# The start of a hybrid encoder layer: how the first operands are loaded, ordered and split

## The chip, the cores and the metric

The kernel runs on one core of a Trainium2 chip. Time is device time in microseconds (us) of one execution of the program; less is better. Engines are named as in the profile: PE is TensorE (PEld its weight loads), DVE VectorE, ACT ScalarE, POOL GpSimd, SP SyncE, which here only issues DMAs. A "q" behind an engine's name is its instruction queue, where DMAs are issued.

## The reference

One layer of a streaming encoder over 512 tokens of width 1024, in float32. Of its three parts (a SwiGLU feed-forward, a mixer of attention and a gated recurrence, a second SwiGLU), only the first is touched here:

```python
def rms_norm(x, g):
    xf = x.astype(jnp.float32)
    y = xf * lax.rsqrt(jnp.mean(xf * xf, axis=-1, keepdims=True) + RMS_EPS)
    return (y * g.astype(jnp.float32)).astype(x.dtype)

def swiglu(x, w1, w3, w2):
    return (jax.nn.silu(x @ w1) * (x @ w3)) @ w2
...
    f = swiglu(rms_norm(h, ffn1_pre_g[l]), ffn1_w1[l], ffn1_w3[l], ffn1_w2[l])
    h = h + 0.5 * rms_norm(f, ffn1_post_g[l])
```

w1 and w3 are 1024 x 2816, w2 is 2816 x 1024.

## The kernel before, in words

Matmuls take two-part operands. Each float32 operand is split into a high part in a reduced format (`fp32r`), made by a copy on ACT, and a low part, the rest, made by a subtraction on DVE. A product is then three matmuls: high x high, low x high and high x low.

**Units.** Columns of w1 and w3 are handled in tiles of 128, each laid out in memory as one 128 x 1024 tile (512 KB): eight blocks k of 128 x 128, one per 128 rows of the weight. A unit is one such tile times the normalized x, transposed: for each k three matmuls of 128 x 512, 24 in all (`mm_feat`, L194). Units come in turns, w1 tile 0, w3 tile 0, w1 tile 1, w3 tile 1 and so on; counted in this `order` from 0, units 0, 1 and 2 are the beginning, unit 3 is w3 tile 1, unit 4 w1 tile 2, unit 5 w3 tile 2. After twelve units the remaining tiles go in pairs through a scheme with fewer products (`Pairs`, L478), whose operands are prepared in parts by `prep`; part 0 makes sums of raw weights (L518 to L521), part 1 splits the first raw tile, part 2 splits sums.

**The norm is applied late.** The first units multiply the weights with x^T scaled by the gain only (`uT`: its high part on ACT, L665, its low part on DVE, L666). The factor of each token comes from the sums of squares of the x rows, which are loaded once more as the residual `h` (four tiles of 512 KB, `h_load`, L94; squares on ACT, L680; the factor in `rstd4`, L244). It is put on diagonals (`dgs`, L686), multiplied with a tile of ones on PE (L700) and copied by ACT to `Rb` (L701). `silu_mul` (L426) then scales the units' results by Rb on DVE.

**The beginning, before.** DVE fills a warm-up tile of 128 x 512 with zeros and PE runs nine matmuls on it (L621 to L625). ACT runs a tiny activation, then issues the load of x^T tile 0 (256 KB, `load_x(0, act)`). SP issues the vector of gains and biases (`vec`), then for each pair of k (kp) a quarter of the raw tiles of units 0, 1 and 2 (128 KB each, `load_w`) and two x^T tiles; for kp = 0 in the order weight 0, weight 1, weight 2, x^T tile 1. Then the raw tiles of units 3 and 4, the four residual tiles and the first two raw tiles of the pairs. The stage at L660 goes through k: for an even k split a quarter of unit 0's weights, scale x^T tile k, split units 1 and 2, and then nine matmuls, three per unit, units in turn.

**Order of the work.** The program order of each engine is as written: every engine takes its queue in order, and what waits holds up all behind it. Tiles live in 42 slots of 4 KB per partition (`slot`); a load into a slot that is in use waits on SP for the slot's last reader. `dma_to(n)` issues the raw loads of all units before n, `split_to(n)` their splits; `get(nm, i, ahead, rawahead)` (L161) asks for both, by default so that two units ahead are split and three more loaded. `point()` runs due work that was put off by `later`.

**After the beginning (L676 to L704), before.** Split units 3 and 4; squares of the four residual tiles; the factor; a tiny activation that brings in the table for Silu; the diagonals; part 0 of the first pair on DVE; then unit 3 through `unit` (its `get` splits unit 5 and requests raw tiles up to unit 8), two small products on PE (one for a table of position biases, whose result `erow` POOL writes to memory as `bias_scr`, L696), the products for Rb, Rb on ACT, parts 1 and 2 of the pair and the first two `silu_mul`.

Of the kernel before, what the change touches and what calls it, by code (L numbers as in the profile page):

```python
# [11 lines left out]
F32R = mybir.dt.float32r  # L12
AF = mybir.ActivationFunctionType
ALU = mybir.AluOpType

P = 128
SEQ = 512
D = 1024
KT = D // P
D_FF = 2816  # L20
FT = D_FF // P
NT = SEQ // P
# [9 lines left out]
V_CW, V_CB, V_BA, V_BX, V_LAM, V_BG, V_G1, V_SINK, V_N = 0, 32, 40, 48, 56, 64, 80, 88, 104  # L32
# [19 lines left out]
def hybrid_layer(ctx: ExitStack, tc: tile.TileContext, a: dict, out: bass.AP):  # L52
    nc = tc.nc
    act, dve, pool, pe, sp = nc.scalar, nc.vector, nc.gpsimd, nc.tensor, nc.sync
# [8 lines left out]
    def slot(shape, dt=F32, name="s"):  # L63
        uid[0] += 1
        return sb.tile(shape, dt, tag="slot", name=f"{name}_{uid[0]}")

    def bank(name="ps"):
        uid[0] += 1
        return pp.tile([P, 512], F32, tag="ps", name=f"{name}_{uid[0]}")
# [5 lines left out]
    def f32(ap):  # L75
        return ap.bitcast(F32)
# [3 lines left out]
    vec = cp.tile([P, V_N], F32, name="vec")  # L80
# [13 lines left out]
    def h_load(src):  # L94
        for t in range(NT):
            h[t] = slot([P, D], name="h")
            sp.dma_start(out=h[t], in_=src[t])
# [51 lines left out]
    def split_to(n):  # L149
        while st["split"] < min(n, len(order)) and st["split"] not in paired:  # L150
            k = st["split"]
            dma_to(k + 1)
            r = raws.pop(k)
            hi = slot([P, D], F32R, name="whi")
            lo = slot([P, D], F32R, name="wlo")
            act.activation(hi, r, AF.Copy)
            dve.tensor_tensor(out=lo, in0=r, in1=f32(hi), op=ALU.subtract)  # L157
            pairs[k] = (hi, lo)
            st["split"] += 1
# [47 lines left out]
    def unit(nm, i, **kw):  # L207
        w = get(nm, i)
        ps = bank("f")
        mm_feat(ps, w, **kw)  # L210
        return ps
# [32 lines left out]
    def rstd4(s4):  # L244

        v, r, e, r2 = (small(NT, x) for x in ("v", "r", "e", "r2"))
        dve.tensor_scalar(out=v, in0=s4, scalar1=D * EPS, scalar2=None, op0=ALU.add)
        act.activation(r, v, AF.Abs_reciprocal_sqrt)
        dve.tensor_tensor(out=e, in0=r, in1=r, op=ALU.mult)
        dve.tensor_tensor(out=e, in0=e, in1=v, op=ALU.mult)  # L250
        dve.scalar_tensor_tensor(out=r2, in0=e, scalar=-3.0, in1=r, op0=ALU.add, op1=ALU.mult)
        return r2, r
# [353 lines left out]
    NS = 3  # L606
# [5 lines left out]
    def load_x(k, q=sp):  # L612
        q.dma_start(out=xts[k // 2][:, k % 2, :], in_=a["xT"][k * P : (k + 1) * P, :])

    def load_w(u, kp):
        nm, i = order[u]
        c = slice(kp * 2 * P, (kp + 1) * 2 * P)
        sp.dma_start(out=raw3[u][:, c], in_=a[nm][i * P : (i + 1) * P, c])


    warm = slot([P, 512], F32R, name="warm")  # L621
    dve.memset(f32(warm), 0.0)
    psw = bank("w")
    for _ in range(WARM):
        pe.matmul(psw, warm[:, :P], warm, start=True, stop=True)  # L625


    tiny = small(4, "tiny")
    dve.memset(tiny, 1.0)
    act.activation(tiny, tiny, AF.Abs_reciprocal_sqrt)  # L630
    load_x(0, act)
    sp.dma_start(out=vec, in_=a["vec"])
    for kp in range(KT // 2):
        load_w(0, kp)
        if kp:
            load_x(2 * kp)
        load_w(1, kp)
        load_w(2, kp)
        load_x(2 * kp + 1)
    dma_to(NS + 2)  # L640
    h_load([a["x"][t * P : (t + 1) * P, :] for t in range(NT)])

    hid, X1 = Hidden(), {}
    pairs_a = Pairs("w1a", "w3a", NC1, X1, hid)
# [12 lines left out]
        hi, lo = pair3[u]  # L657
        split2(hi[:, c], lo[:, c], raw3[u][:, c])

    for k in range(KT):  # L660
        if k % 2 == 0:
            split_first(0, k // 2)
        g = vec[:, V_G1 + k : V_G1 + k + 1]
        xk = xts[k // 2][:, k % 2, :]
        act.activation(uT[:, 0, k, :], xk, AF.Copy, scale=g)  # L665
        dve.scalar_tensor_tensor(out=uT[:, 1, k, :], in0=xk, scalar=g, in1=f32(uT[:, 0, k, :]), op0=ALU.mult, op1=ALU.subtract)  # L666
        if k % 2 == 0:
            split_first(1, k // 2)
            split_first(2, k // 2)
        s_ = slice(k * P, (k + 1) * P)  # L670
        for (hi, lo), p_ in zip(pair3, ps):
            pe.matmul(p_, hi[:, s_], uT[:, 0, k, :], start=k == 0, stop=False)
            pe.matmul(p_, lo[:, s_], uT[:, 0, k, :], start=False, stop=False)
            pe.matmul(p_, hi[:, s_], uT[:, 1, k, :], start=False, stop=k == KT - 1)
    del raw3, pair3, hi, lo
    split_to(NS + 2)  # L676
    s4 = small(NT, "s4")
    for t in range(NT):
        junk = slot([P, D], name="junk")
        act.activation(junk, h[t], AF.Square, accum_out=s4[:, t : t + 1])  # L680

    r, q = rstd4(s4)
    act.activation(tiny, q, AF.Silu)
    dgs = slot([P, NT, P], name="dgs")
    for t in range(NT):
        dve.tensor_scalar(out=dgs[:, t, :], in0=ident, scalar1=r[:, t : t + 1], scalar2=NEWT, op0=ALU.mult, op1=ALU.mult)  # L686
    pairs_a.prep(0, 0, dve)
    ps.append(unit("w3a", 1))

    pse = bank("e")  # L690
    pe.matmul(pse[:N_HEADS, : NREL + 1], oh[:, NREL + 1 :], oh[:, : NREL + 1], start=True, stop=True)
# [7 lines left out]
    for t in range(NT):  # L699
        pe.matmul(psr[:, t * P : (t + 1) * P], ones, dgs[:, t, :], start=True, stop=True)  # L700
    act.activation(Rb, psr, AF.Copy)  # L701
    pairs_a.prep(0, 1)
    hid.f += [silu_mul(ps[0], ps[1], Rb), silu_mul(ps[2], ps[3], Rb)]
    pairs_a.prep(0, 2)  # L704
# [226 lines left out]
    for i in range(8):  # L931
        ps = unit("wg", i)
# [261 lines left out]

CONV_AT = (0, 1, 2, 4, 5, 6, 8, 10)
RG_AT = (7, 11, 13, 15, 17, 19, 21, 23)
WARM = 9
ATT_STEP = 2.2
ATT_LAG = (1, 1, 4, 1, 3, 1)
RG_LAG = 2  # L1200
# [63 lines left out]
```

## Time and profile before

| | |
|---|---|
| median of three executions | 1135.56 us (1135.35 to 1135.70) |
| the profiled execution | 1135.67 us |
| its span, first to last instruction | 1133.8 us |
| mean granted PE clock | 0.998 |

An engine's rows read: start and length in us, engine, line, operation, tiles written and read, shapes, and in brackets the engine's idle time before it and what ended that. A row of the stretches gives the stretch, its length, then the busy time of PE, PEld, DVE, ACT and POOL with instruction counts, the granted clock, the share of the DMA engines in use and GB/s. A row of waits names who waited for whom: us in total, times, longest. A row of DMA issues ends with the number of issues, the size of one and the us from issue to landing.

### The profile page before, as it was taken

What the parts mean: (1) busy time and instruction counts of PE and PEld (TensorE: products, weight loads), DVE (VectorE), ACT (ScalarE), POOL (GpSimd) and SP (SyncE); (2) the same over time, 40 slices, a digit from 0 to 9 for tenths busy, and PEclk for the clock granted to TensorE, in tenths of its full rate; (3) what the DMA queues carried; (4) which work ended last, traced back from release to release, by engine and by line L of the source; (5) the groups of instructions that cost most, each with busy time, mean ns of one, the idle gap of its engine ahead of it and who ended that gap; (6) DMA issues with size and microseconds to landing.
All of it is one profiled execution on the core that took longest, in us unless ns stands there. A gap on an engine that the chain in (4) does not pass through costs nothing.

```text
span 1133.8 us, 17339 instructions
## 1 busy us (share of the span) xinstructions
PE 1125.3 (99%) x6763; PEld 1003.5 (89%) x6763; DVE 790.1 (70%) x1181; ACT 585.2 (52%) x1042; POOL 353.8 (31%) x265
## 2 busy tenths in 40 slices
PE   9999999999999999999999999999999999999997
PEld 7889999988889987888888888889999999998886
DVE  5997889885436747695678865767899777975313
ACT  6445555574324349844655663356555555574211
POOL 0148678500000000001555643000965566700000
PEclk9999999999999999999999999999999999999999
DMA  9953223264313311234122333531323332255101
GB/s 343 157 135 112 93 95 112 76 222 151 110 56 135 144 56 57 75 95 148 56 78 90 93 95 112 185 111 38 113 94 94 112 112 76 94 197 172 40 19 56
DMA packets 36945, 124.94 MB, mean 110 GB/s; under 512 B 4416, under 2 KB 6208, under 8 KB 36864
## 3 DMA queue, kind: packets, MB, share of 16 engines
q1 hardware_dynamic: 34272, 115.15, 30.3%
q0 software_dynamic: 2448, 8.43, 4.0%
q8 instruction: 53, 0.87, 0.3%
q10 hardware_dynamic: 144, 0.26, 0.1%
q14 instruction: 28, 0.23, 0.1%
HBM read 116.50 MB, written 7.33 MB: 109 GB/s over the span
## 4 chain that ended last, share of the span: by engine, by line
PE 93%; DVE 3%; ACT 2%; issue 1%; DMA 0%; SPq 0%; DVEq 0%
PE c L475 11%; PE c L474 11%; PE c L473 11%; PE f L202 10%; PE f L201 10%; PE f L203 10%; PE acc L220 8%; PE acc L221 8%; PE acc L219 8%; PE pt L1067 1%; PE s L1031 1%; PE s L1030 1%; PE tr L310 1%; PE o L1083 1%; PE o L1084 1%
## 5 line engine op out<-in xcount | busy, mean ns | idle before, releaser
L201 PE MATMUL f<-uT,whi 128*128 128x512 f32 (+1 forms) x504 | 184.2, 365 | 0.0
L202 PE MATMUL f<-uT,wlo 128*128 128x512 f32 (+1 forms) x504 | 183.0, 363 | 0.4 <-DVE wlo L157 0.3
L203 PE MATMUL f<-uT,whi 128*128 128x512 f32 (+1 forms) x504 | 182.6, 362 | 0.0
L219 PE MATMUL acc<-whi,hT 128*128 128x512 f32 x352 | 137.1, 390 | 0.0
L220 PE MATMUL acc<-wlo,hT 128*128 128x512 f32 x352 | 137.0, 389 | 0.0
L221 PE MATMUL acc<-whi,hT 128*128 128x512 f32 x352 | 136.9, 389 | 0.0
L474 PE MATMUL c<-Xh,wlo 128*128 128x256 f32 x432 | 122.3, 283 | 0.0
L475 PE MATMUL c<-Xl,whi 128*128 128x256 f32 x432 | 122.3, 283 | 0.0
L473 PE MATMUL c<-uT,whi 128*128 128x256 f32 x432 | 122.3, 283 | 0.0
L474 PE MATMUL c<-uT,wlo 128*128 128x256 f32 x432 | 122.3, 283 | 0.0
L475 PE MATMUL c<-uT,whi 128*128 128x256 f32 x432 | 122.3, 283 | 0.0
L473 PE MATMUL c<-Xh,whi 128*128 128x256 f32 x432 | 122.3, 283 | 0.0
L192 DVE TENSOR_TENSOR wlo<-S,whi 128x1024 fp32r<-128x1024 f32 x72 | 118.2, 1642 | 3.6 <-ACT whi L191 3.2
L202 PEld LDWEIGHTS f<-uT,wlo 128*128 128x128 f32 x504 | 95.2, 189 | 15.8 <-DVE wlo L157 1.6
L201 PEld LDWEIGHTS f<-uT,whi 128*128 128x128 f32 x504 | 95.1, 189 | 15.8 <-issue 1.4
L203 PEld LDWEIGHTS f<-uT,whi 128*128 128x128 f32 x504 | 95.1, 189 | 14.8
L473 PEld LDWEIGHTS c<-Xh,whi 128*128 128x128 f32 x432 | 82.9, 192 | 0.0
L474 PEld LDWEIGHTS c<-Xh,wlo 128*128 128x128 f32 x432 | 82.9, 192 | 0.0
L473 PEld LDWEIGHTS c<-uT,whi 128*128 128x128 f32 x432 | 82.9, 192 | 0.0
L474 PEld LDWEIGHTS c<-uT,wlo 128*128 128x128 f32 x432 | 82.9, 192 | 0.0
L475 PEld LDWEIGHTS c<-uT,whi 128*128 128x128 f32 x432 | 82.9, 192 | 0.0
L475 PEld LDWEIGHTS c<-Xl,whi 128*128 128x128 f32 x432 | 82.9, 192 | 0.0
(309 smaller groups left out, 2703.8 us busy)
## 6 DMA issues: line engine op xcount, KB each, us to landing
raw_w2a<-in_w2a_dram SPq DMA_DIRECT2D x22, 512.0 KB, 3.7
raw_w1b<-in_w1b_dram SPq DMA_DIRECT2D x22, 512.0 KB, 4.2
raw_w3b<-in_w3b_dram SPq DMA_DIRECT2D x22, 512.0 KB, 4.2
raw_w2b<-in_w2b_dram SPq DMA_DIRECT2D x22, 512.0 KB, 4.1
raw_w3a<-in_w3a_dram SPq DMA_DIRECT2D x21, 512.0 KB, 4.5
raw_w1a<-in_w1a_dram SPq DMA_DIRECT2D x20, 512.0 KB, 4.5
raw_wg<-in_wg_dram SPq DMA_DIRECT2D x16, 512.0 KB, 3.7
raw_xr<-in_xr_dram SPq DMA_DIRECT2D x8, 512.0 KB, 4.7
```

What stands on the lines that cost most here:

```text
L192: dve.tensor_tensor(out=lo, in0=src, in1=f32(hi), op=ALU.subtract)
L201: pe.matmul(ps[:, c0:c1], wh[:, s], h_, start=k == 0, stop=False)
L202: pe.matmul(ps[:, c0:c1], wl[:, s], h_, start=False, stop=False)
L203: pe.matmul(ps[:, c0:c1], wh[:, s], l_, start=False, stop=k == KT - 1)
L219: pe.matmul(acc[n], x[:, 0, c], wh[:, s], start=first, stop=False)
L220: pe.matmul(acc[n], x[:, 0, c], wl[:, s], start=False, stop=False)
L221: pe.matmul(acc[n], x[:, 1, c], wh[:, s], start=False, stop=last)
L310: pe.transpose(ps[:, k * P : (k + 1) * P], hg[:, kk * P : (kk + 1) * P], ident)
L473: pe.matmul(ps, wh[:, s], xh, start=first, stop=False, skip_group_check=True)
L474: pe.matmul(ps, wl[:, s], xh, start=False, stop=False, skip_group_check=True)
L475: pe.matmul(ps, wh[:, s], xl, start=False, stop=k == 3, skip_group_check=True)
L1030: pe.matmul(o, lq, KS[g][:, 0, k0 : k0 + n], start=True, stop=False)
```

## The change

The warm-up tile becomes 128 x 128, is filled by POOL, and is read four times over as the moving operand of the warm-up matmuls, of which there are seven. x^T tile 0 is loaded in two column halves, one issued by SP, one by ACT, ahead of everything else; `vec` goes behind the half on ACT. x^T tile 1 goes ahead of weight 2; in later rounds the first x^T tile goes ahead of all three weights. The residual tiles are requested ahead of unit 4's raw tile.

For k = 0 the steps are written out: x's high part first on ACT; unit 0's weights wholly on DVE (the copy too); units 1 and 2's high parts on ACT; the nine matmuls in another order. From k = 1 the order is as before.

Behind the beginning, only unit 3 is split ahead of the squares; unit 4 is split behind the factor, unit 5 behind Rb; unit 3's `get` looks one unit ahead instead of two.

```diff
-    warm = slot([P, 512], F32R, name="warm")
-    dve.memset(f32(warm), 0.0)
+    warm = slot([P, P], F32R, name="warm")
+    pool.memset(f32(warm), 0.0)
     psw = bank("w")
+    wide = bass.AP(tensor=warm.tensor, offset=warm.offset, ap=[warm.ap[0], [0, 4], [1, P]])
     for _ in range(WARM):
-        pe.matmul(psw, warm[:, :P], warm, start=True, stop=True)
-
+        pe.matmul(psw, warm, wide, start=True, stop=True)
+
+
+    for q, c0 in ((sp, 0), (act, 256)):
+        q.dma_start(out=xts[0][:, 0, c0 : c0 + 256], in_=a["xT"][:P, c0 : c0 + 256])
+    act.dma_start(out=vec, in_=a["vec"])
 
     tiny = small(4, "tiny")
     dve.memset(tiny, 1.0)
     act.activation(tiny, tiny, AF.Abs_reciprocal_sqrt)
-    load_x(0, act)
-    sp.dma_start(out=vec, in_=a["vec"])
     for kp in range(KT // 2):
-        load_w(0, kp)
         if kp:
             load_x(2 * kp)
+        load_w(0, kp)
         load_w(1, kp)
+        if not kp:
+            load_x(1)
         load_w(2, kp)
-        load_x(2 * kp + 1)
+        if kp:
+            load_x(2 * kp + 1)
+    dma_to(NS + 1)
+    h_load([a["x"][t * P : (t + 1) * P, :] for t in range(NT)])
     dma_to(NS + 2)
-    h_load([a["x"][t * P : (t + 1) * P, :] for t in range(NT)])
...
-    for k in range(KT):
+    def x_hi(k):
+        act.activation(uT[:, 0, k, :], xts[k // 2][:, k % 2, :], AF.Copy, scale=vec[:, V_G1 + k : V_G1 + k + 1])
+
+    def x_lo(k):
+        dve.scalar_tensor_tensor(
+            out=uT[:, 1, k, :], in0=xts[k // 2][:, k % 2, :], scalar=vec[:, V_G1 + k : V_G1 + k + 1],
+            in1=f32(uT[:, 0, k, :]), op0=ALU.mult, op1=ALU.subtract)
+
+    def mm_first(k, u, w, x):
+        pe.matmul(
+            ps[u], pair3[u][w][:, k * P : (k + 1) * P], uT[:, x, k, :],
+            start=k == 0 and w == x == 0, stop=k == KT - 1 and x == 1)
+
+
+    (hi0, lo0), c = pair3[0], slice(0, 2 * P)
+    x_hi(0)
+    dve.tensor_copy(hi0[:, c], raw3[0][:, c])
+    dve.tensor_tensor(out=lo0[:, c], in0=raw3[0][:, c], in1=f32(hi0[:, c]), op=ALU.subtract)
+    for u in (1, 2):
+        act.activation(pair3[u][0][:, c], raw3[u][:, c], AF.Copy)
+    x_lo(0)
+    for u in (1, 2):
+        dve.tensor_tensor(out=pair3[u][1][:, c], in0=raw3[u][:, c], in1=f32(pair3[u][0][:, c]), op=ALU.subtract)
+    for u, w, x in ((0, 0, 0), (0, 1, 0), (1, 0, 0), (2, 0, 0), (0, 0, 1), (1, 0, 1), (2, 0, 1), (1, 1, 0), (2, 1, 0)):
+        mm_first(0, u, w, x)
+    for k in range(1, KT):
         if k % 2 == 0:
             split_first(0, k // 2)
-        g = vec[:, V_G1 + k : V_G1 + k + 1]
-        xk = xts[k // 2][:, k % 2, :]
-        act.activation(uT[:, 0, k, :], xk, AF.Copy, scale=g)
-        dve.scalar_tensor_tensor(out=uT[:, 1, k, :], in0=xk, scalar=g, in1=f32(uT[:, 0, k, :]), op0=ALU.mult, op1=ALU.subtract)
+        x_hi(k)
+        x_lo(k)
         if k % 2 == 0:
             split_first(1, k // 2)
             split_first(2, k // 2)
-        s_ = slice(k * P, (k + 1) * P)
-        for (hi, lo), p_ in zip(pair3, ps):
-            pe.matmul(p_, hi[:, s_], uT[:, 0, k, :], start=k == 0, stop=False)
-            pe.matmul(p_, lo[:, s_], uT[:, 0, k, :], start=False, stop=False)
-            pe.matmul(p_, hi[:, s_], uT[:, 1, k, :], start=False, stop=k == KT - 1)
-    del raw3, pair3, hi, lo
-    split_to(NS + 2)
+        for u in range(NS):
+            for w, x in ((0, 0), (1, 0), (0, 1)):
+                mm_first(k, u, w, x)
+    del raw3, pair3, hi0, lo0
+    split_to(NS + 1)
     s4 = small(NT, "s4")
     for t in range(NT):
         junk = slot([P, D], name="junk")
         act.activation(junk, h[t], AF.Square, accum_out=s4[:, t : t + 1])
 
     r, q = rstd4(s4)
+    split_to(NS + 2)
     act.activation(tiny, q, AF.Silu)
...
     pairs_a.prep(0, 0, dve)
-    ps.append(unit("w3a", 1))
+    w = get("w3a", 1, ahead=1)
+    ps.append(bank("f"))
+    mm_feat(ps[3], w)
...
     act.activation(Rb, psr, AF.Copy)
+    split_to(NS + 3)
     pairs_a.prep(0, 1)
...
-WARM = 9
+WARM = 7
```

## The prediction, before the changed kernel was run

> **What bounds the kernel now.** I read the page's shares and chain first, then the stretches and the waits of TensorE (PE), then the first 10 us row by row.
>
> ```profile
> PE 1125.3 (99%) x6763; PEld 1003.5 (89%) x6763; DVE 790.1 (70%) x1181; ACT 585.2 (52%) x1042; POOL 353.8 (31%) x265
> ...
> PE 93%; DVE 3%; ACT 2%; issue 1%; DMA 0%; SPq 0%; DVEq 0%
> ```
> ```profile
> 28.30:40.00 11.70, 11.70 (x56) 9.32 (x56) 10.70 (x14) 7.99 (x11) 1.03 (x1) 1.00 0.96 195
> 40.00:60.00 20.00, 19.70 (x87) 16.02 (x86) 19.83 (x29) 6.05 (x7) 2.40 (x1) 1.00 0.97 126
> 60.00:100.00 40.00, 40.00 (x280) 37.54 (x279) 35.04 (x35) 21.62 (x33) 25.77 (x14) 1.00 0.42 125
> ```
> ```profile
> PE w L625 <- DVE tiny L629: 1.4, 1, 1.4
> PE f L202 <- DVE wlo L157: 0.3, 1, 0.3
> ```
>
> PE is busy 99% and holds 93% of the chain. In the stretches (length, then busy time of PE, weight load, DVE, ACT, POOL) the reader should see that only the first 60 us matter: from 60 to 100 us PE has no gap. And between 28 and 60 us DVE is as full as PE (10.70 of 11.70, 19.83 of 20.00). PE's list of waits has two rows: before its first matmul, and once for a low half made by DVE. So a microsecond won at the start reaches the end only if DVE arrives a microsecond earlier at that second row.
>
> The start, from the timeline:
>
> ```profile
> 0.73 0.39 SPq L632 DMA_DIRECT2D vec<-in_vec_dram  x1
> ...
> 1.18 0.42 SPq L618 DMA_DIRECT2D raw_first<-in_w1a_dram  x1
> ...
> 1.45 4.21 PE L625 MATMUL w<-warm 128*128 128x512 f32 x9 [1.45 <-DVE tiny L629]
> 1.46 0.37 ACTq L613 DMA_DIRECT2D xt<-in_xT_dram  x1
> ...
> 2.59 0.43 SPq L613 DMA_DIRECT2D xt<-in_xT_dram  x1
> ...
> 3.79 0.42 ACT L191 ACTIVATE whi<-raw_first 128x256 fp32r<-128x256 f32 x1 [1.57 <-DMA raw_first<-in_w1a_dram]
> ...
> 4.62 0.72 ACT L665 ACTIVATE uT<-xt,vec 128x512 fp32r<-128x512 f32 x1 [0.42 <-DMA xt<-in_xT_dram]
> ...
> 5.46 0.74 PE L672 MATMUL f<-uT,whi 128*128 128x512 f32 x1
> ...
> 6.60 0.39 PE L672 MATMUL f<-uT,whi 128*128 128x512 f32 x1
> ...
> 6.83 0.40 PE L673 MATMUL f<-uT,wlo 128*128 128x512 f32 x1
> ...
> 7.14 0.72 ACT L665 ACTIVATE uT<-xt,vec 128x512 fp32r<-128x512 f32 x1 [1.10 <-DMA xt<-in_xT_dram]
> ...
> 7.90 0.75 DVE L666 SCALAR_TENSOR_TENSOR uT<-xt,vec,uT 128x512 fp32r<-128x512 f32 x1 [1.09 <-ACT uT L665]
> ...
> 9.05 0.40 PE L672 MATMUL f<-uT,whi 128*128 128x512 f32 x1
> ```
>
> The first useful matmul starts at 5.46, when x's high half is made (4.62 + 0.72). Nine warm-ups take 4.21 us, at most 0.47 each; from 6.60 to 6.83 the step is 0.23. I number the useful matmuls from 0: number 12, at 9.05, is the first after which PE has no gap until 57 us. **Its place is the measure of the start**: what it gains, PE gains up to 57 us.
>
> **The change at the start.** Issue to landing, each row from the DMA view of a window about one issue:
>
> ```profile
> vec<-in_vec_dram SPq DMA_DIRECT2D x1, 52.0 KB, 1.8
> ```
> ```profile
> xt<-in_xT_dram ACTq DMA_DIRECT2D x1, 256.0 KB, 3.1
> raw_first<-in_w1a_dram SPq DMA_DIRECT2D x1, 128.0 KB, 2.6
> ```
> ```profile
> raw_first<-in_w3a_dram SPq DMA_DIRECT2D x1, 128.0 KB, 3.3
> raw_first<-in_w1a_dram SPq DMA_DIRECT2D x1, 128.0 KB, 3.5
> ```
>
> SP's first five issues (0.73 to 2.59) stand 0.46 us apart. Before: vec 0.73, weight 0 at 1.2, weight 1 at 1.65, weight 2 at 2.1, x tile 1 at 2.6; x tile 0 goes out on ACT at 1.46. After: SP sends half of x 0 at 0.73, weight 0 at 1.2, weight 1 at 1.65, x 1 at 2.1, weight 2 at 2.6; ACT sends the other half at 0.73 and vec at about 1.1, then loads its table, which ends about 2.9 and hides behind the landings.
>
> Half a tile alone is bounded by vec's 1.8 us below and the whole tile's 3.1 above: x 0 lands between 2.5 and 3.8. I take 3.5, nearer the upper row, because both halves are under way together. vec now lies behind a half: 2.9 to 4.2 by the same two rows, I take 3.7, and that starts the scaling of x, 0.9 us earlier than 4.62. Weight 0 lands as before, 3.8, or a little later beside the halves: 4.0.
>
> [...]
>
> DVE now makes weight 0's high half. There is no row of that copy at this size; the nearest is twice as wide:
>
> ```profile
> L849 DVE CAST xcs<-xc_t x8: 418/420/423, 396.9 to 451.4; 128x512 fp32r<-128x512 f32 x8
> ```
>
> So 0 to 0.42 us, I take 0.35: ready at 4.35, the low half 0.42 later; x's high half at 3.7 + 0.72 = 4.42. **Matmul 0 starts about 4.5**, 0.9 earlier, still at the slow rate; 1 and 2 follow to 5.4. Matmul 3 needs the high half of weight 2, and PE takes its queue in order. Weight 2 has gone behind x 1: 948 KB are now issued up to and including it, just what was issued before up to x 1, which landed at 7.1 (the wait of ACT's row at 7.14 ends with it); when 128 KB less x 1 lay ahead, it landed at 5.6 (2.1 + 3.5). These are the bounds, 5.6 and 7.1. The flow now begins earlier with full transfers and weight 2 is half of x 1's size, so I take the lower end, 5.8. ACT's copy (0.42) gives matmul 3 at 6.25, then nine steps of 0.23 to number 12, and a little for the end of the slow rate: 8.4. By the other limit, ACT scales x 1 from 6.2 to 6.9, DVE's low half takes 0.75, so number 11 can start at 7.7 and does not bind. **PE's gain at number 12: 9.05 - 8.4 = 0.65 us**; by the bounds 0.85 to -0.55.
>
> The smaller warm tile costs nothing visible: POOL fills 128x128 where DVE filled 128x512.
>
> ```profile
> 0.73 0.20 POOL masks.py:197 MEMSET ident<- 128x128 f32 x1 [0.29 <-POOLq L1252]
> ```
>
> Warm-ups begin about 1.0 instead of 1.45; seven of them end about 4.2, before matmul 0. Identity and the ones tile go 0.2 us later on POOL; their readers are the diagonals and products just ahead of Rb.
>
> **The change at 16 to 58 us.** The rows on which it hangs:
>
> ```profile
> 27.38 0.69 DVE L518 TENSOR_TENSOR S<-raw_w1a 128x512 f32<-128x512 f32 x1 [0.87 <-DMA raw_w1a<-in_w1a_dram]
> ...
> 28.61 1.06 ACT L156 ACTIVATE whi<-raw_w3a 128x1024 fp32r<-128x1024 f32 x1 [2.15 <-DMA raw_w3a<-in_w3a_dram]
> ...
> 30.05 1.22 DVE L157 TENSOR_TENSOR wlo<-raw_w3a,whi 128x1024 fp32r<-128x1024 f32 x1
> 30.18 0.60 ACT L701 ACTIVATE Rb<-r 128x512 f32<-128x512 f32 x1
> 30.34 1.03 POOL L696 DMA_DIRECT2D bias_scr<-erow  x1 [27.64 <-ACT erow L693]
> 30.67 1.05 ACT L191 ACTIVATE whi<-raw_w1a 128x1024 fp32r<-128x1024 f32 x1
> 31.76 1.23 DVE L192 TENSOR_TENSOR wlo<-raw_w1a,whi 128x1024 fp32r<-128x1024 f32 x1 [0.50 <-ACT whi L191]
> 32.90 0.69 DVE L433 TENSOR_TENSOR sw<-f,Rb 128x512 f32<-128x512 f32 x1
> ...
> 47.13 1.23 DVE L157 TENSOR_TENSOR wlo<-raw_w1a,whi 128x1024 fp32r<-128x1024 f32 x1
> ...
> 56.63 1.22 DVE L157 TENSOR_TENSOR wlo<-raw_w3a,whi 128x1024 fp32r<-128x1024 f32 x1
> ...
> 57.90 0.50 PE L202 MATMUL f<-uT,wlo 128*128 128x512 f32 x1 [0.30 <-DVE wlo L157]
> ```
> ```profile
> 31.70:57.90 26.20, 25.90 (x115) 21.12 (x114) 25.50 (x37) 11.10 (x14) 2.40 (x1) 1.00 0.97 125
> ```
>
> The residual tiles move ahead of weight tile 4 (units counted from 0), so the squares on ACT and the factor come about 1.2 us earlier; but the factor's consumer waits for PE anyway. Tile 4's split moves behind it, to about 24 to 26 us; PE needs it only after the product that Rb copies (30.18 - 0.65). Both cost nothing. In DVE's queue tile 4's split delays the diagonals by 1.2 us, before the sums at 27.38 that wait for a DMA: hidden.
>
> The step that costs is **tile 5's split**, moved behind Rb. Before, DVE made its low half at 30.05 to 31.27, in time that it would otherwise have idled, since the next product waited for Rb and a copy on ACT until 31.76. After, ACT makes Rb, then tile 5's high half, then the pair's; DVE waits from about 30 until tile 5's copy, at 31.76 - 0.65, makes its low half there, and only then the pair's. One step of this kind is 1.14 us (31.76 to 32.90). Behind it DVE is full to the row that PE waits for: 25.50 of 26.20 us. Nothing there can take up 1.14 us. So the low half at 56.63 comes 1.14 - 0.65 = 0.49 us later, and PE, which already waited for it, with it. From there PE is without a gap, so the end moves as that matmul does.
>
> **Sum:** span 1133.8 + 0.49 = 1134.3; the profiled execution took 1135.67, 1.87 more than its span and 0.11 above the median 1135.56. On the median: 1135.56 + 0.49, **1136.1 us**. It is not measurable: 0.2% (2.3 us), about what a measurement of this kernel can tell from no change, is four times as much.
>
> **Rivals.**
> (a) *DVE's delay is absorbed.* For it: DVE idles 0.70 us in that window. Against: the idle parts follow ACT work that moves along. PE would keep its 0.65: 1134.9.
> (b) *Weight 2 lands late*, the start does not do what it says. At 7.1, matmul 3 starts at 7.55 and number 12 at 9.6: 0.55 lost, plus 1.14: 1137.25. For it: the bytes ahead; against: the earlier flow.
> (c) *The slow rate lasts longer.* Here the rate rose by 6.60, 5.15 us after the first warm-up. PE now idles about 0.3 us before matmul 0 and 0.8 before matmul 3. If the count began anew at matmul 0, the slow rate would hold to 9.65; from 6.25 on half of 3.4 us is lost, 1.7, and 0.49 + 1.7 gives 1137.75. It decides from 0.65 us of lost rate on, where it outweighs the gain at the start. [...] The trace agrees with a change of rate, with 0.23 us after 6.60; whether a short gap resets it no row shows.
> (d) *A tile is caught behind the bias transfer.* One weight load issued at 33.0 beside it took
>
> ```profile
> raw_w3a<-in_w3a_dram SPq DMA_DIRECT2D x1, 512.0 KB, 23.4
> ```
>
> to land. That transfer now starts some 1.2 us earlier, since its row no longer queues behind the copy at 28.61, and tile 8 is requested one call later. Tile 8's low half is DVE's row at 47.13. If tile 8, issued at about 24, took as long, it would land at 47.4 and with ACT's copy (1.06) delay that row by 1.3 us: 1137.4; if it landed with the quoted one, at 56.4, by ten: 1146. Against: it is issued some 5 us before the transfer.
>
> **How the numbers follow.** Forecast 0.48 (its own range 1135.4 to 1136.9), (a) 0.24, (b) 0.13, (c) 0.11, (d) 0.04. The range takes in (a), (b) and the lower part of (c), 1134.6 to 1137.7; it leaves out half of (c), (d), and the lowest fifth of (a). Slower by over 0.2% begins at 1137.83: (d), half of (c) and a little of (b), 0.11. Faster by over 0.2% (below 1133.3) would need both the whole gain and the removal of the stall at 57 us with more: 0.03. Within: 0.86.
>
> **What would show it.** Matmul 0 near 4.5 and a gap before matmul 3 that a DMA of the third weight ends; number 12 near 8.4; DVE idle before tile 5's low half near 31; PE's wait at the tenth unit grown from 0.3 to about 1.5 us. If that wait has not grown, the DVE step was wrong; if number 12 is later than 9, the start was.

## The result and the profile after

The changed kernel took 1139.36 us (median of six executions, 1138.67 to 1140.9), the kernel before 1135.34 us on the same chip (1135.03 to 1135.7): a ratio of 1.0037, 95% interval 1.0024 to 1.005. The change costs 4.0 us, where 0.5 had been predicted. The profiled execution is the longest of the six, 1140.9 us, with a span of 1139.0 us, 5.2 more than the profiled one before; what follows in this section accounts for those 5.2 us.

The busy row and the chain of the page after, and TensorE's waits in the first 300 us (who waited for whom: us in total, times, longest):

```profile
PE 1127.2 (99%) x6761; PEld 1004.8 (88%) x6761; DVE 790.6 (69%) x1181; ACT 584.7 (51%) x1041; POOL 354.0 (31%) x266
...
PE 93%; DVE 3%; ACT 2%; issue 1%; DMA 0%; SPq 0%; DVEq 0%
```
```profile
PE f L676 <- ACT whi L686: 1.8, 2, 1.6
PE f L202 <- DVE wlo L157: 1.4, 1, 1.4
PE w L626 <- POOL warm L622: 1.0, 1, 1.0
PE f L676 <- ACT uT L668: 1.0, 1, 1.0
```

PE is still the bound. But two rows are new: 1.0 us for x's high part and 1.8 us for high parts of weights. Before, PE had no wait at all between its first warm-up and 57 us. The wait at the tenth unit has grown from 0.3 to 1.4.

The start row by row, from the timeline after:

```profile
0.99 3.29 PE L626 MATMUL w<-warm 128*128 128x512 f32 x7 [0.99 <-POOL warm L622]
...
4.46 0.72 ACT L668 ACTIVATE uT<-xt,vec 128x512 fp32r<-128x512 f32 x1 [1.31 <-DMA vec<-in_vec_dram]
5.24 0.50 PE L676 MATMUL f<-uT,whi 128*128 128x512 f32 x1 [0.96 <-ACT uT L668]
5.69 0.42 ACT L686 ACTIVATE whi<-raw_first 128x256 fp32r<-128x256 f32 x1 [0.50 <-DMA raw_first<-in_w3a_dram]
6.16 0.50 PE L676 MATMUL f<-uT,whi 128*128 128x512 f32 x1 [0.18 <-ACT whi L686]
7.79 0.42 ACT L686 ACTIVATE whi<-raw_first 128x256 fp32r<-128x256 f32 x1 [1.69 <-DMA raw_first<-in_w1a_dram]
8.26 2.08 PE L676 MATMUL f<-uT,whi 128*128 128x512 f32 x4 [1.60 <-ACT whi L686]
```

Matmul 0 starts at 5.24, only 0.22 us earlier than before: x is scaled from 4.46 on, when the vector of gains lands. Matmul 2 waits for weight 1, matmul 3 for weight 2, which lands at 7.77; matmul 3 starts at 8.26, where before it started at 6.60. That is 1.66 us of the loss. The DMA view of windows about single issues after (issues, size, us from issue to landing) has the landings:

```profile
xt<-in_xT_dram ACTq DMA_DIRECT2D x1, 128.0 KB, 3.0
xt<-in_xT_dram SPq DMA_DIRECT2D x1, 128.0 KB, 2.8
vec<-in_vec_dram ACTq DMA_DIRECT2D x1, 52.0 KB, 3.2
raw_first<-in_w3a_dram SPq DMA_DIRECT2D x1, 128.0 KB, 4.0
raw_first<-in_w1a_dram SPq DMA_DIRECT2D x1, 128.0 KB, 5.2
```

Weight 1 (w3a) is issued at 1.65 as before, but takes 4.0 us where it took 3.3. Weight 2, the last row, took 3.5 before and 5.2 now, and is issued half a microsecond later.

The rest of the start's loss lies behind matmul 3. Five stretches after (length, then busy time of PE, weight load, DVE, ACT and POOL with counts, granted clock, share of the DMA engines, GB/s):

```profile
0.99:4.07 3.08, 3.08 (x7) 2.15 (x7) 0.00 (x0) 1.49 (x2) 1.69 (x5) 1.00 0.69 175
4.07:7.49 3.42, 1.44 (x4) 0.48 (x3) 1.90 (x4) 1.14 (x2) 0.00 (x0) 1.00 0.94 295
7.49:10.90 3.41, 2.64 (x6) 2.16 (x7) 2.47 (x6) 3.11 (x7) 0.00 (x0) 0.50 1.02 335
10.90:14.31 3.41, 3.41 (x9) 2.65 (x8) 3.41 (x9) 3.28 (x8) 0.00 (x0) 0.50 0.97 313
14.31:33.00 18.69, 18.69 (x82) 14.75 (x80) 8.87 (x19) 9.80 (x17) 0.00 (x0) 1.00 0.92 367
```

The granted clock is recorded as raised at 4.07 (ahead of the first record the column shows 1.00, though the warm-ups step at 0.43 us, the slow rate). From 4.07 to 7.49 PE is busy 1.44 of 3.42 us; at 7.49 the clock falls to 0.50 and stays there through the next two rows, 6.82 us, the first of which still holds the end of the wait for weight 2, until 14.31. Before, the one rise came at 6.30, and the clock did not fall until the last 5 us of the span. In PE's rows one can see the rate by the step from start to start:

```profile
13.12 1.05 PE L676 MATMUL f<-uT,whi 128*128 128x512 f32 x2
13.97 0.56 PE L676 MATMUL f<-uT,wlo 128*128 128x512 f32 x1
14.37 0.62 PE L676 MATMUL f<-uT,whi 128*128 128x512 f32 x2
14.83 0.39 PE L676 MATMUL f<-uT,wlo 128*128 128x512 f32 x1
```

0.43 us up to 13.97, 0.23 from 14.37 on. Unit 3 starts at 26.84 instead of 22.71: 4.13 us, of which 1.66 are matmul 3's delay and the other 2.47 come behind it, where 14 steps run at the slow rate: 14 x 0.20 = 2.8, less the 0.4 that PE had lost before to short gaps between its matmuls 3 and 12. Number 12, the measure of the start, comes at 12.27 instead of 9.05.

The later part, from the timeline after:

```profile
34.31 0.60 ACT L732 ACTIVATE Rb<-r 128x512 f32<-128x512 f32 x1 [0.61 <-PE r L731]
34.81 1.05 ACT L156 ACTIVATE whi<-raw_w3a 128x1024 fp32r<-128x1024 f32 x1
35.89 1.23 DVE L157 TENSOR_TENSOR wlo<-raw_w3a,whi 128x1024 fp32r<-128x1024 f32 x1 [6.12 <-ACT whi L156]
37.03 1.22 DVE L192 TENSOR_TENSOR wlo<-raw_w1a,whi 128x1024 fp32r<-128x1024 f32 x1
38.17 0.68 DVE L433 TENSOR_TENSOR sw<-f,Rb 128x512 f32<-128x512 f32 x1
...
61.89 1.22 DVE L157 TENSOR_TENSOR wlo<-raw_w3a,whi 128x1024 fp32r<-128x1024 f32 x1
63.16 0.50 PE L202 MATMUL f<-uT,wlo 128*128 128x512 f32 x1 [1.43 <-DVE wlo L157]
```

Everything is 4.13 later (Rb at 34.31 instead of 30.18), and DVE's row with Rb at L433 comes at 38.17 instead of 32.90, 5.27 later: the split of unit 5 stands between. PE's row at 63.16 is 5.26 later than before, and so is the end, within 0.1 us.

So three things cost: weight 2 lands late, the clock falls, and one split moved into DVE's full stretch. The theory is that these three, which hang on three separate edits or sizes, make the whole loss. The rivals: that one of them is all of it, or that an earlier start of the loads gains nothing here whatever its order.

### The profile page after: what moved, and what is told of

Its sections match the earlier page's. It is cut to its first block, busy times and chain, and to the rows that moved or that the text cites. A ratio compares the mean times of both kernels' runs of the same rounds, so it can differ in the third digit from the quotient of the medians.

```text
span 1139.0 us, 17334 instructions
## 1 busy us (share of the span) xinstructions
PE 1127.2 (99%) x6761; PEld 1004.8 (88%) x6761; DVE 790.6 (69%) x1181; ACT 584.7 (51%) x1041; POOL 354.0 (31%) x266
## 3 DMA queue, kind: packets, MB, share of 16 engines
q0 software_dynamic: 2448, 8.43, 3.9%
## 4 chain that ended last, share of the span: by engine, by line
PE 93%; DVE 3%; ACT 2%; issue 1%; DMA 0%; SPq 0%; DVEq 0%
PE c L475 11%; PE c L474 11%; PE c L473 11%; PE f L202 10%; PE f L201 10%; PE f L203 10%; PE acc L220 8%; PE acc L221 8%; PE acc L219 8%; PE f L676 2%; PE pt L1099 1%; PE s L1063 1%; PE s L1062 1%; DVE wlo L157 1%; PE tr L310 1%
```

## The experiments

Each was timed in five rounds beside the kernel before, whose median stood between 1135.26 and 1135.42 us in all of them. All compute the whole layer; where matmuls of zeros are added, their bank is read by nothing.

### The two parts apart

**e1_back_alone**: the kernel before with the edits behind the beginning only.

```diff
+    dma_to(NS + 1)
     h_load([a["x"][t * P : (t + 1) * P, :] for t in range(NT)])
+    dma_to(NS + 2)
...
-    split_to(NS + 2)
+    split_to(NS + 1)
...
     r, q = rstd4(s4)
+    split_to(NS + 2)
...
     act.activation(Rb, psr, AF.Copy)
+    split_to(NS + 3)
```

> Only the later part of the change, on the kernel before: residual ahead of unit 4's raw tile, unit 4 split behind the factor, unit 5 behind Rb. Theory (the 4.0 us are a sum of two things, this one and the start): 1.1 us slower than before, matmuls of the start unmoved, Rb unmoved at 30.2, DVE's low half for unit 5 at 31.8 instead of 30.05 and PE's wait at the tenth unit grown from 0.3 to 1.4. Rival (the delay on DVE is absorbed when PE does not come late, and all 4.0 us are the start's): within 0.3 us of before.

1136.47 us, 1.14 more than the kernel before (ratio 1.001, 1.0001 to 1.0019). Its timeline and waits:

```profile
31.17 1.22 DVE L157 TENSOR_TENSOR wlo<-raw_w3a,whi 128x1024 fp32r<-128x1024 f32 x1 [1.71 <-ACT whi L156]
```
```profile
PE f L202 <- DVE wlo L157: 1.4, 1, 1.4
```

DVE idles 1.71 us ahead of unit 5's low half, which it made at 30.05 before, and PE waits 1.4 at the tenth unit. The edits behind the beginning cost what was predicted, and the two rows put it at this step.

**e2_front_alone**: the change with those edits undone.

> Only the first part of the change: halves, load order, warm-up and first matmuls as changed, the splits behind it as before. Theory (sum): 2.9 us slower than before, 1.1 faster than the change, PE's wait at the tenth unit back at 0.3 to 0.5. Rival (the start's loss makes the later part cost more, or the late part alone explains it): as slow as the change, 4 us over before, or no slower than before.

1137.59 us, 2.26 more (1.0013 to 1.0033); less than the 2.9 that were expected. The executions lie in two groups, five from 1137.2 to 1137.6 and four from 1138.3 to 1138.9. PE's wait at the tenth unit is back to 0.4, and matmul 3 starts at 7.41. The start alone is a loss.

**e9_change_again**: the change once more, timed beside e6, e7 and e8.

> The change itself once more, beside the others on the same chip, for the mends to be compared with. [...]

1139.05 us (1137.32 to 1140.12; ratio 1.0033, 1.002 to 1.0045). The change spreads by 2.8 us over five executions; of 27 of the kernel before, 26 lie within 0.9 us and one stands apart at 1137.21. With these five, the change has eleven executions, and their median is 1139.15 us.

### The start's costs, taken away one at a time

**e4_weight2_first**: weight 2 ahead of x^T tile 1.

```diff
         load_w(1, kp)
-        if not kp:
-            load_x(1)
         load_w(2, kp)
-        if kp:
-            load_x(2 * kp + 1)
+        load_x(2 * kp + 1)
```

> The change with weight 2 ahead of x tile 1 again, nothing else. Theory (matmul 3 waits for weight 2, which lands behind x 1 at 7.8 instead of 5.6): weight 2 lands near 6.2, matmul 3 near 6.7 instead of 8.26; 1.5 us faster than the change, or 3 us if PE's clock no longer drops at 7.5. Rival (the transfers all land late because of the halves and the vector on ACT's queue, whatever their order): weight 2 lands after 7, less than 0.7 us gained.

1137.89 us (1.0014 to 1.0032), 1.5 less than the change (1.3 less than the median of its eleven executions). Two rows of its timeline:

```profile
6.16 0.72 ACT L683 ACTIVATE whi<-raw_first 128x256 fp32r<-128x256 f32 x2 [1.22 <-DMA raw_first<-in_w3a_dram]
6.63 1.65 PE L673 MATMUL f<-uT,whi 128*128 128x512 f32 x3 [0.41 <-ACT whi L683]
```

Now ACT waits once and copies weights 1 and 2 in one go; matmul 3 starts at 7.22 instead of 8.26. But weight 1 lands at 6.14, later than in the change, so the order of the two is not the whole delay. Matmul 3 had been expected near 6.7.

**e5_fill**: the change's loads, with nine warm-ups and six more matmuls of zeros between the useful matmuls 2 and 3, so that PE is not idle while it waits.

```diff
-WARM = 7
+WARM = 9
+FILL = 6
...
+        if (u, w, x) == (2, 0, 0):
+            for _ in range(FILL):
+                pe.matmul(psw, warm, wide, start=True, stop=True)
         mm_first(0, u, w, x)
```

> The change with PE kept busy: nine warm-ups instead of seven, and six more matmuls on zeros between useful matmuls 2 and 3, where PE idled; their results are not read. Theory (the slow rate from 7.5 to 14.3 in the profile comes from PE's idle time before it): the clock stays up, matmul 3 still near 8.3, the step behind it 0.23 instead of 0.43; 1.5 to 2 us faster than the change. Rival (the clock has its own time and idle gaps play no part): no gain, or a loss by the fillers.

1137.87 us (1.0015 to 1.0033), 1.5 less than the change (1.3 by the eleven); ten of its executions lie within 0.6 us, one at 1139.96. Timeline and stretches:

```profile
6.71 0.50 PE L676 MATMUL f<-uT,whi 128*128 128x512 f32 x1 [0.91 <-ACT whi L686]
7.05 1.54 PE L693 MATMUL w<-warm 128*128 128x512 f32 x6
8.43 1.07 PE L676 MATMUL f<-uT,whi 128*128 128x512 f32 x4
```
```profile
4.90:8.40 3.50, 2.59 (x10) 1.72 (x10) 1.88 (x4) 1.88 (x5) 0.00 (x0) 1.00 1.02 347
8.40:14.00 5.60, 5.60 (x26) 4.63 (x25) 5.56 (x12) 5.12 (x12) 0.00 (x0) 1.00 1.02 352
```

This is the cleanest of the experiments: matmul 3 starts at 8.43, even later than in the change, but PE is busy 2.59 of 3.50 us in the stretch ahead of it, the clock stays up, and 26 matmuls fit into 5.60 us. What was won is the clock's share alone, and work that computes nothing won it: the six fillers, and the two more warm-ups, which take away the wait ahead of matmul 0. The two were not tried apart.

**e6_before_warm7**: the kernel before with seven warm-ups instead of nine.

```diff
-WARM = 9
+WARM = 7
```

> The kernel before with seven warm-ups instead of nine, nothing else. PE would then idle about 0.9 us before useful matmul 0. [...] Rival (a gap of under 1 us does not matter): median and spread as before, within 0.2 us.

1136.66 us (1135.43 to 1137.23; ratio 1.0011, 1.0002 to 1.0019). The profiled execution, one of the quick ones, shows PE waiting 1.0 us for x with the clock up at 4.43 and staying (from 4.43 to 7.84 nine matmuls take 2.36 busy us). The slower ones were not profiled; that the clock fell in them is argued, not shown.

**e7_x0_whole**: x^T tile 0 as one transfer on ACT; SP then begins with weight 0, and all its loads go out one issue (0.46 us) earlier.

```diff
-    for q, c0 in ((sp, 0), (act, 256)):
-        q.dma_start(out=xts[0][:, 0, c0 : c0 + 256], in_=a["xT"][:P, c0 : c0 + 256])
+    load_x(0, act)
     act.dma_start(out=vec, in_=a["vec"])
```

> The change with x tile 0 as one transfer of 256 KB on ACT's queue instead of two halves; everything else as in the change. Theory (each transfer of 128 rows takes its turn, so one transfer less ahead of them brings weights 1 and 2 earlier): weight 1 lands at 5.0 to 5.3 instead of 5.7 to 6.2, weight 2 about 0.4 earlier than the 6.9 to 7.8 of the change, x 0 about as before; 0.3 to 0.8 us faster than the change. Rival (the order by bytes decides): weights land as in the change, within 0.2 us, and the time is the change's within 0.4.

1136.64 us (1.0008 to 1.0026), 2.4 less than the change, far more than expected. The whole tile lands at 4.0, 0.2 later than the halves; but weight 2, issued at 2.11, lands at 5.83, and x^T tile 1 at 5.45. From the DMA view of its issue, then two stretches of its trace:

```profile
raw_first<-in_w1a_dram SPq DMA_DIRECT2D x1, 128.0 KB, 3.7
```
```profile
3.36:6.78 3.42, 2.31 (x6) 1.40 (x5) 2.07 (x5) 1.96 (x4) 0.00 (x0) 1.00 1.07 368
6.78:10.19 3.41, 3.41 (x9) 2.63 (x9) 2.17 (x6) 1.80 (x5) 0.00 (x0) 1.00 0.93 272
```

3.7 us to landing instead of 5.2, and PE has no gap behind matmul 0. The executions lie at 1136.3 to 1136.6 (six) and 1137.9 to 1138.5 (five); the means of the groups are 1.8 us apart, about what a stretch of 3.41 us at the slow rate costs (eight steps of 0.43 instead of 0.23 us: 1.6); that the clock makes the groups is argued, since only one execution, of the upper group, was profiled. Its clock first rises at 10.19, at the end of the full stretch and not of the one ahead of it, in which the wait for x left PE busy 2.31 of 3.42 us (the column shows 1.00 ahead of the first record here too; nine matmuls in 3.41 us are the slow rate; the stretch of e5 at the fast one holds 26 in 5.60).

**e13_halves_on_act**: both halves on ACT, so that SP's loads also go out earlier.

```diff
-    for q, c0 in ((sp, 0), (act, 256)):
+    for q, c0 in ((act, 0), (act, 256)):
```

> The change with both halves of x tile 0 issued by ACT, so that SP's first transfer is weight 0 again, as in the run with x 0 whole. Theory (the half on SP delays every transfer that SP issues behind it by one place, and that is what the change pays): weight 1 lands near 4.5 and weight 2 near 6, as with x 0 whole; 2 us or more faster than the change. Rival (the number of transfers counts, one of 128 rows more): weights land as in the change, weight 2 after 7, less than 0.7 us gained.

1139.6 us (1.0024 to 1.0051): the expectation missed. The weights do land earlier (weight 1 at 4.68, weight 2 at 6.45), but the vector of gains is now third in ACT's queue, is issued at 1.65 and lands at 6.2:

```profile
6.31 0.72 ACT L668 ACTIVATE uT<-xt,vec 128x512 fp32r<-128x512 f32 x1 [2.68 <-DMA vec<-in_vec_dram]
7.09 0.51 PE L676 MATMUL f<-uT,whi 128*128 128x512 f32 x1 [2.77 <-ACT uT L668]
```

One gap of 2.77 us before matmul 0 costs about as much as the change's three: the clock rises at 4.16, falls at 7.57 and returns at 10.98.

**e8_three_mends**: unit 5's split early again, weight 2 ahead of x^T tile 1, nine warm-ups and two fillers ahead of matmul 2.

> The change with three mends at once: unit 5 split ahead of Rb as before, weight 2 ahead of x tile 1 as before, and PE kept busy by nine warm-ups and two more zero matmuls ahead of useful matmul 2 (not read). Theory (the three losses add up and there is no other): the change's excess of 4.0 goes away, 1135.0 to 1135.8, PE's wait at the tenth unit 0.3 to 0.4. Rival (halves and the vector behind them cost something of their own): still 0.7 us or more over before.

1135.76 us (0.9995 to 1.0013), 0.5 more than the kernel before. Its waits:

```profile
PE f L202 <- DVE wlo L157: 0.3, 1, 0.3
PE f L673 <- ACT uT L665: 0.2, 1, 0.2
```

With the three costs taken away, 0.5 of the 4.0 us are left, and the interval of the ratio takes in none. Singly, they gave 1.5 (e4), 1.5 (e5) and, from e2, 1.8: 4.8 for a loss of 4.0. An overlap is to be expected, since an earlier weight 2 also shortens PE's idle time, but its size is not shown: by the change's eleven executions the three give 4.1 for a loss of 3.8.

### Is there a gain to be had from the early start?

**e10_early_x0**: the kernel before with the load of x^T tile 0 issued ahead of ACT's tiny activation. **e11_early_x0_warm**: the same, with the change's warm-up tile and ten warm-ups. **e12_vec_sp_x0_act**: the change with unit 5's split early, weight 2 first, x^T tile 0 whole on ACT, the vector first on SP and ten warm-ups.

```diff
+    load_x(0, act)
     tiny = small(4, "tiny")
     dve.memset(tiny, 1.0)
     act.activation(tiny, tiny, AF.Abs_reciprocal_sqrt)
-    load_x(0, act)
     sp.dma_start(out=vec, in_=a["vec"])
```

> The kernel before with one edit: x tile 0's load on ACT ahead of the tiny activation, so issued at 0.73 instead of 1.46. Theory (matmul 0 waits for x 0, and PE's rate is still slow there): x 0 lands 0.5 to 0.7 earlier, matmul 0 at 4.9 to 5.1, 0.1 to 0.5 us faster than before. Rival (the table load, now behind the issue, or weights 0 to 2, pushed back by x 0, take it away): within 0.1 of before, or slower.

> The same, and the small warm-up tile filled by POOL, with ten warm-ups from 1.0 that reach to 5.3. Theory (an earlier unbroken stretch of PE work brings the clock up earlier): the rise moves up by up to 0.5 us on the mean, 0.1 to 0.3 us faster than the run without it. Rival (ten warm-ups overrun matmul 0 by 0.3): same or up to 0.2 slower.

> What is left of the change when its losing parts are taken back: the small warm-up tile with ten warm-ups, x 0 whole on ACT at 0.73 and the vector first on SP, the first matmuls by readiness of operands with weight 0 split on DVE, residual ahead of unit 4's tile; weight 2 ahead of x 1 and unit 5's split as before. Theory: matmul 0 at 4.7 to 4.9, no gap over 0.4 behind it, 0.3 to 0.8 us faster than before. Rival (the first matmuls' order brings nothing beside an early x 0): the same as the run with early x 0 and early warm-ups, within 0.15.

1135.55 (0.9992 to 1.001), 1135.74 (0.9993 to 1.0011) and 1136.03 us (0.9997 to 1.0014): no gain, and all three theories missed. In e10 x lands at 3.84 instead of 4.54, but weight 1 at 6.01 instead of 4.93 and weight 2 at 6.28 instead of 5.60. That is not what held PE: as before, its list has no wait between the first warm-up and the tenth unit. Matmul 0 starts at 5.45, as before, for two other reasons. ACT copies weight 0 first, which lands at 4.17 instead of 3.77, so x is scaled from 4.51, only 0.11 earlier; and the nine warm-ups run to 5.66. The prediction reads matmul 0's start before, at 5.46, off x's high half alone; the warm-ups hold it as well. In e12, too, they run to 5.62 and matmul 0 starts at 5.42 without a wait. So e10 and e12 do not try what a much earlier matmul 0 would bring.

**e14_change_pool_late, e15_early_x0_warm_pool_late, e16_vec_sp_pool_late, e17_before_pool_late**: POOL's two small loads (the one-hot table, 48 KB, and the bias table, 2 KB, issued at 1.54 and 2.23 in the change) are held until x^T tile 2 has landed; in the change, in e11, in e12 and in the kernel before.

```diff
+    hold = small(4, "hold")
+    pool.tensor_scalar(out=hold, in0=xts[1][:, 0, :4], scalar1=1.0, scalar2=None, op0=ALU.mult)
     pool.dma_start(out=oh[:, : NREL + 1], in_=a["onehot"])
```

> The change, with POOL's two small loads (one-hot rows and bias table, 50 KB) held back until x tile 2 has landed; a tiny POOL operation waits for it. Theory (these loads share the engines just when weights 1 and 2 are due): weight 1 lands near 4.5 to 5 instead of 5.7 to 6.3, weight 2 near 6.5 instead of 6.9 to 7.8, 0.8 to 2 us faster than the change. Rival (the flow is slow there for the number of small transfers or their order, POOL's loads play no part): weights land as in the change, time within 0.5 of it.

> The kernel before with x 0 issued at 0.73, the small warm-up tile with ten warm-ups, and POOL's loads held back. Theory: weight 1 by 4.6 and weight 2 by 5.6 in every execution, 0.3 to 0.7 us faster than before. Rival: as without holding back, 0 to 0.4 over before.

> What is left of the change (x 0 whole on ACT, vector first on SP, first matmuls by readiness, ten early warm-ups, old places for weight 2 and unit 5's split), and POOL's loads held back. Theory: weight 2 lands near 5.7 instead of 6.8, no gap before matmul 3, 0.3 to 0.8 us faster than before. Rival: 0.4 us or more over before, as without holding back.

> The kernel before with POOL's two small loads held back in the same way. Theory (they take part of the flow at 4 to 5 us): weights 1 and 2 and x 1 land 0.2 to 0.6 earlier, 0 to 0.4 us faster. Rival: unchanged, within 0.15.

e14: 1137.83 us (1.0014 to 1.0032), 1.5 under the change; x^T tile 1 lands at 6.09 and weight 2 at 6.43 in its trace, 1.36 and 1.34 earlier than in the change's, and matmul 3 starts at 6.92. Its executions reach from 1136.65 to 1139.86, so they overlap with the change's, and against the median of the change's eleven the gain is 1.3. e15, e16 and e17: 1135.48, 1135.94 and 1135.26 us, all within 0.1% of the kernel before and of the kernels that they were made from. The theories of e15 and e16, 0.3 to 0.8 us under the kernel before, missed. So holding the small loads back probably helped the change, where the first loads are late, and showed no effect elsewhere.

**e19_weight0_first**: the change, but SP sends weight 0 first and its half of x^T tile 0 second.

```diff
+    load_w(0, 0)
     for q, c0 in ((sp, 0), (act, 256)):
...
-        load_w(0, kp)
+        if kp:
+            load_w(0, kp)
```

> The change, but SyncE issues weight 0 first and its half of x tile 0 second. In all kernels so far in which x tile 0 goes out at 0.73 and SyncE's first issue is not a weight, the loads move 151 to 242 GB/s between 3.5 and 4.7 us; in the two in which it is weight 0 (e7, e13) 380 and 291. If the first place of the weight is what keeps the flow up, this run shows 290 GB/s or more there, weight 1 landed by 5.1 and the time 1 to 2 us under the change, about 1137.5. The rival, that it hangs on how many bytes the two engines have issued by 1.2 us (436 KB in the change and here, 512 and 564 KB in e13 and e7), expects 180 GB/s or less, weight 1 after 5.4 and about 1139.

1139.47 us (1.002 to 1.0043): as the change. Between 3.5 and 4.7 us the loads moved 216 GB/s, and weight 1 landed at 6.09. What goes first on SP is not what matters; the theory behind this run falls. The rival's 180 GB/s or less was not met either, though its time was.

**e18_best**: the change with x^T tile 0 whole on ACT (as e7), weight 2 first (as e4), unit 5's split early and ten warm-ups.

> The change with x tile 0 whole on ScalarE, so that SyncE begins with weight 0 (as in e7), weight 2 ahead of x tile 1, unit 5 split early, and ten warm-up matmuls, which end about 5.2 and so leave no gap before the first useful matmul. The theory that the loss is three separate costs (a late weight 2, a clock that falls, the moved split) expects matmul 0 at 5.4 to 5.5, no gap behind it, the clock up from about 4.4 on, number 12 about 8.3 and so 0.3 to 0.8 us under the kernel before: 1134.6 to 1135.1. The rival, that an earlier stream of loads on two queues always gives back what it gains, expects 1135.3 to 1136.2.

1135.2 us (1134.98 to 1135.41; ratio 0.9998, 0.9989 to 1.0007). PE's waits and the stretch that held the change's idle time:

```profile
PE w L626 <- POOL warm L622: 1.0, 1, 1.0
PE f L202 <- DVE wlo L157: 0.4, 1, 0.4
```
```profile
4.07:7.49 3.42, 3.42 (x12) 2.25 (x11) 2.42 (x6) 2.31 (x6) 0.00 (x0) 1.00 1.00 342
```

Weight 2 lands at 5.00, PE is busy throughout, matmul 0 starts at 5.61, when the ten warm-ups end (0.99 + 4.64), and number 12 at 8.45, 0.6 earlier than before. Its span is 1133.2 us, 0.6 under the one profiled before, so number 12 is again the measure. But the medians are 0.19 us apart, 0.1 above the upper end of what was expected and 0.1 below the lower end of the rival's range, and the kernel before varies by 0.75 us from one execution to the next: 4.2 us are won on the change, and on the kernel before nothing that the measurement can tell.

## Why the prediction was wrong, step by step

**Right: DVE's step.** Unit 5's split behind Rb costs 1.14 us: e1 measured 1.14, and the wait at the tenth unit came out at 1.43 (1.5 foretold). The moves of the residual and of unit 4's split cost nothing, and no tile was caught behind the bias transfer: tile 8's low half stands at 52.40, 5.27 after 47.13, as all of DVE's work behind Rb. Rivals (a) and (d) are out.

**Wrong: "I take the lower end, 5.8" for weight 2's landing.** The bounds were 5.6 and 7.1; it landed at 7.77 in the profiled execution and 7.52 in e9, beyond the upper bound, and matmul 3, put at 6.25, started at 8.26 and 8.01. The argument was that the flow begins earlier. It does, and then it slumps. The same stretch of the kernel before, of e10 (the kernel before with x sent at 0.73) and of e7:

```profile
3.50:4.70 1.20, 1.20 (x5) 0.91 (x4) 0.43 (x1) 0.49 (x2) 0.00 (x0) 1.00 1.03 360
```
```profile
3.50:4.70 1.20, 1.20 (x5) 0.91 (x4) 0.06 (x1) 0.51 (x2) 0.00 (x0) 1.00 0.87 177
```
```profile
3.50:4.70 1.20, 0.84 (x2) 0.12 (x1) 0.72 (x2) 0.02 (x1) 0.00 (x0) 1.00 1.07 380
```

And of the change and of e14:

```profile
3.50:4.70 1.20, 0.78 (x2) 0.12 (x1) 0.50 (x2) 0.24 (x1) 0.00 (x0) 1.00 0.76 155
```
```profile
3.50:4.70 1.20, 0.85 (x2) 0.13 (x1) 0.72 (x2) 0.59 (x1) 0.00 (x0) 1.00 0.92 151
```

The last two columns tell it: in the change the DMA engines are in use 0.76 of the time and move 155 GB/s, where they moved 360 before at full use. They stand idle for a part of the stretch, and a packet takes longer: by the DMA view of this stretch, SP's queue (q1 there) has 116 packets in 45.1% of 16 engines' 1.2 us, about 75 ns each, where it had 216 in 48.3%, about 43 ns each, before, and the packets are of nearly the same size (1.1 and 0.9 KB). Bytes issued ahead, by which the bounds were set, say nothing of that.

**Wrong, smaller: x and the vector.** The halves landed at 3.55 and 3.78 (3.5 taken), the vector at 4.35 (3.7 taken, 4.2 the bound), so matmul 0 came at 5.24 and not at 4.5. In e9 the halves landed at 3.28 and 3.46, nearer to the 3.5 taken.

**Wrong: the clock, which the forecast put at next to nothing.** The prediction saw PE idle for 0.3 us before matmul 0 and 0.8 before matmul 3, and its sum holds no more for that than "a little for the end of the slow rate"; a longer slow rate was only rival (c). In the execution profiled after the change PE idled for 0.96 and 0.18 + 1.60 us; the clock rose early, at 4.07, and fell again at 7.49, behind 3.42 us of which PE was idle for 1.98. The trace of e9, of an execution that at 1139.67 us lies nearer to the median, shows the form that (c) has: one rise, late, at 12.20. Its stretches:

```profile
8.01:12.20 4.19, 4.19 (x10) 3.32 (x11) 4.00 (x9) 4.15 (x10) 0.00 (x0) 1.00 0.99 339
12.20:17.00 4.80, 4.80 (x23) 3.94 (x22) 4.31 (x9) 3.30 (x8) 0.00 (x0) 1.00 0.95 323
```

Ten matmuls in 4.19 us, then 23 in 4.80 (ahead of the first record the clock's column shows 1.00 here too). There matmul 3 starts at 8.01, 1.41 later than before, and unit 3 at 25.75, 3.04 later, so that the slow rate takes 1.63 us, where (c) had 1.7; with DVE's 1.1 that is the 4.1 us by which its span is longer. In e5, with the gap filled (PE busy 2.59 of 3.50 us), the clock stayed up: here the idle time is the cause. In the change's trace the fall comes 3.42 us behind the first rise and the next rise 6.82 behind the fall; by what rule the clock rises and falls is not shown.

**Wrong: the rivals as alternatives.** (b), weight 2 late, and (c), a longer slow rate, had 0.13 and 0.11 and 1137.25 and 1137.75 us. But here late data made PE idle (2.7 us in all in the change's profiled execution, 1.7 in e9), and the clock fell behind it, at 7.49, or rose late, at 12.20: the second followed from the first. By the prediction's own numbers both together are 1137.25 + 1.7 = 1138.95 us, 0.4 from the median; in e9's trace both came true. That case was not on the list, and the range ended below it.

**Open.** Why the flow slumps between 3.5 and 4.7 us. It is not the halves (e10 sends the tile whole and has 177 GB/s), not POOL's loads (e14: 151), and not what SP sends first (e19: 216), each tried alone. Of the kernels that send x at 0.73, those with 436 KB issued by 1.2 us have 151 to 242 GB/s there, those with 512 KB or more (e13, e7, e18) 291 to 381; but the kernel before, with less than either, has 360, so this is an observation and not yet a cause.

## What to carry to other kernels

Before a load is moved ahead, ask when the loads behind it will land: in the change and in e10, x landed 0.7 to 1.0 us earlier and weights 1 and 2 0.7 to 2.2 us later, and in the change the operand that landed last set the start. It need not go so: in e7 and e18 SP begins with weight 0; in e7 x landed 0.5 us earlier, and weight 2 landed at 5.83 and 5.00, where it had landed at 5.60 before. When a prediction finds a new gap on TensorE near the beginning, price the clock along with it, in one case: here gaps of 1.7 us in all (e9) and 2.7 (the change's profiled execution) cost 1.6 and 2.5 us more through the slow rate, and dummy matmuls that filled them won about 1.3 to 1.5 back (e5). Do not take work out of an engine's idle time (the split of unit 5 ahead of Rb) to put it where the engine is full: here that cost 1.14 us (e1).

## What the hardware showed that was not expected

- The granted clock fell after a stretch in which PE was busy 1.44 of 3.42 us (42%), while it stayed up over one with 2.59 of 3.50 (74%, e5). It had not come back at 10.90, behind 2.64 busy of 3.41 us (77%); it came back at 14.31, behind 3.41 of 3.41. The busy share alone does not settle the first rise: it came at 4.43 behind 2.98 of 3.41 us in e6 (87%), and not behind 3.15 in e19 (5.99 to 9.40, 92%).
- Executions of one kernel differed more where PE idled near the beginning: from lowest to highest 2.2 and 2.8 us in the change, 2.2 in e7, 3.2 in e14, 1.3 in e13 (five executions). With PE busy throughout, e18 spreads by 0.43 us. There are exceptions: e12, with a wait of 0.6 us, spreads by 0.68, and the kernel before had its one execution at 1137.21.
- The same 128 KB load, issued at the same 1.65 us by the same engine, landed after 3.3 us in the kernel before and after 4.0 in the change (4.6 in e9); 52 KB took 1.8 us at the head of SP's queue and 4.55 in third place on ACT's (e13, 1.65 to 6.20).
